# Small tiles move to the constants pool, and the pools behind start at one address offset

## The chip, the cores and the metric

The kernel runs on one core of a Trainium2 chip. The metric is device time in microseconds (us) of one execution, from launch to end; lower is better. The profile shows one execution of the same program, instruction by instruction.

## What is computed

One decoder layer on 512 tokens of width 1024, in float32, plus a final norm:

```
h = x + 0.5 * SwiGLU(RMSNorm(h))            # d_ff 2816
u = RMSNorm(h);  P = u @ W_in               # short conv, Mamba-2 and gate columns
y_a = W_out_a(b * conv3(c * v))
y_b = W_out_ssm(GroupRMSNorm(SSD(conv4(xBC)) * silu(z)))     # 32 heads, 4 groups, chunks of 128
h = h + W_mix_out(sigmoid(g_a) * y_a + sigmoid(g_b) * y_b)
h = h + CrossAttn(RMSNorm(h), RMSNorm(mem))                  # 4 heads, 256 memory tokens
h = h + 0.5 * SwiGLU(RMSNorm(h))
out = RMSNorm(h)
```

## The kernel before

Everything is held transposed: channels on the 128 partitions, the 512 tokens along the free axis. So a tile of one 128-channel block is 128x512 float32, which is 2048 bytes per partition. The output of every weight product is built in PSUM 128 channels at a time.

**The inner loop.** Nearly all of TensorE's time goes to `job` (lines 99 to 112). It computes one 128-channel block of `x @ W`: for each of the k blocks of input channels, a 128x128 block of the weights is the stationary operand and an activation tile of 128x512 is the moving one. To get float32 precision out of the faster float32r matmuls, both operands are split into a high and a low part, and each k block takes three matmuls: high weights with high activations (line 110), high weights with low activations (line 111) and low weights with high activations (line 112). `load_w` (lines 86 to 97) brings 128x1024 weights by DMA (`wr`), ScalarE rounds them to the high part (`wh`, line 84) and VectorE subtracts for the low part (`wl`, line 85); three buffers of each rotate in the pool `wp`.

**The moving tiles** have names that tell the stage. `uh`/`ul` are the layer input with its gain (pool `up`; both feed-forward gate/up products, the projection `w_in`, and the queries). `sh`/`sl` are the SwiGLU products (pool `fp`; both down projections). `ynh`/`ynl` are the normed SSD outputs (pool `mx`; `w_os`). `yah`/`yal` and `mgh`/`mgl` are the short-conv output and the merged branches (pool `mb`; `w_oa` and `w_mo`). `mnh`/`mnl` are the memory tokens (256 wide; `w_k`). For `w_v` (lines 516 to 518) the roles are turned: 512 columns of weights move and `mnh`/`mnl` are stationary. `kh`/`kl` move and `qh`/`ql` are stationary in the attention scores (lines 559 to 561), `ph`/`pl` move against `vh`/`vl` (lines 598 to 600), and `oh`/`ol` are the attention outputs (pool `xo`; `w_o`). The last block of the second down projection is done in two halves of 256 tokens (`finish`, lines 650 to 652).

**Memory.** Pools are laid out one behind the other in SBUF, in the order in which they are opened: `cst` (constants), `wp` (weights), then `up` (u tiles) and `wk` (work tiles `sq`, `sd`, `rc`, `r`, `sdf`), then the pool of the stage (`fp`, `mo` with `mx` or `mb`, `xa` with `xn` or `xo`). The residual tiles `h` sit at the other end. A tile takes its bytes per partition, rounded up to 32. All large tiles are multiples of 1 KB, so a small tile shifts everything behind it: in `wk`, two `sd` and two `rc` buffers (16 bytes, rounded to 32) stand in front of `r` and `sdf` (64 bytes) behind it; in `xo`, four `mxs` buffers (32 bytes) stand in front of `e`, `ph`, `pl`, `oh` and `ol`.

**The order of work** is that of the program on each engine: no instruction is placed by a planner at run time. TensorE works through jobs, with the small products of the SSD and of the norms between them.

Of the kernel before, what the change touches and what calls it, by code (L numbers as in the profile page):

```python
# [16 lines left out]
F32 = mybir.dt.float32  # L17
# [5 lines left out]
P = 128  # L23
# [24 lines left out]
def layer(ctx: ExitStack, tc: tile.TileContext, a, out):  # L48
# [4 lines left out]
    cst = ctx.enter_context(tc.tile_pool(name="cst", bufs=1))  # L53
# [8 lines left out]
    def nm(s):  # L62
        uid[0] += 1
        return f"{s}_{uid[0]}"

    def ps(tag="pj"):
        return psp.tile([P, T], F32, tag=tag, name=nm(tag), bufs=PJ if tag == "pj" else 8 - PJ)
# [7 lines left out]
    eps = cst.tile([P, 1], F32, tag="eps", name="eps")  # L75
    V.memset(eps, EPS)

    ahead = []

    def pc(name, i):  # L80
# [6 lines left out]
    def load_w(src, n, parts=1):  # L87
        if ahead:
            return ahead.pop(0)
        raw = wp.tile([P, 1024], F32, tag="wr", name=nm("wr"), bufs=3)  # L90
        hi = wp.tile([P, 1024], F32R, tag="wh", name=nm("wh"), bufs=3)
        lo = wp.tile([P, 1024], F32R, tag="wl", name=nm("wl"), bufs=3)
        for i in range(parts):
            c = slice(i * n // parts, (i + 1) * n // parts)
            nc.sync.dma_start(out=raw[:, c], in_=src[:, c])
            split(raw[:, c], hi[:, c], lo[:, c])
        return hi, lo
# [25 lines left out]
    def rms(tiles, n, pool, n_tok=T):  # L123


        nt = n_tok // P
        acc = None
        for k, t in enumerate(tiles):
            sq = pool.tile([P, T], F32, tag="sq", name=nm("sq"), bufs=3)[:, :n_tok]
            S.activation(out=sq, in_=t, func=AF.Square)  # L130
            if acc is None:
                acc = sq
            else:
                V.tensor_tensor(out=sq, in0=acc, in1=sq, op=ALU.add)  # L134
                acc = sq
        p1 = ps("ss")
        for c in range(nt):
            TE.matmul(p1[:, c:c + 1], acc[:, c * P:(c + 1) * P], ones[:, 0:1], start=True, stop=True)
        sd = pool.tile([P, 4], F32, tag="sd", name=nm("sd"), bufs=2)[:, :nt]
        S.activation(out=sd, in_=p1[:, :nt], func=AF.Sqrt, scale=1.0 / n, bias=eps)  # L140
        rc = pool.tile([P, 4], F32, tag="rc", name=nm("rc"), bufs=2)[:, :nt]
        V.reciprocal(out=rc, in_=sd)
        rb = pool.tile([P, T], F32, tag="sq", name=nm("rb"), bufs=3)[:, :n_tok]
        V.tensor_copy(out=rb.rearrange("p (c t) -> p c t", c=nt),
                      in_=rc.unsqueeze(2).to_broadcast([P, nt, P]))
        p2 = ps("ss")
        for c in range(nt):
            TE.transpose(p2[:, c * P:(c + 1) * P], rb[:, c * P:(c + 1) * P], ident)
        r = pool.tile([P, T], F32, tag="r", name=nm("r"), bufs=2)[:, :n_tok]
        S.copy(out=r, in_=p2[:, :n_tok])  # L150
        return r
# [12 lines left out]
    wk = ctx.enter_context(tc.tile_pool(name="wk", bufs=1, reuse_waits="tile"))  # L164
# [325 lines left out]
    with tc.tile_pool(name="xa", bufs=1, reuse_waits="tile") as xa:  # L490
# [36 lines left out]
        with tc.tile_pool(name="xo", bufs=1, reuse_waits="tile") as xo:  # L527
            def xt(tag, bufs, shape=(P, T), dt=F32):
                return xo.tile(list(shape), dt, tag=tag, name=nm(tag), bufs=bufs)
# [19 lines left out]
            def scores(hd, qs):  # L549
                pp = [ps("ss") for _ in range(2)]  # L550
                probs = []
                for c2 in range(2):
                    sc = pp[c2]
                    for cc in range(2):
                        cs = slice((2 * c2 + cc) * P, (2 * c2 + cc + 1) * P)
                        o_ = sc[:, cc * M:(cc + 1) * M]
                        for j in range(2):
                            (qh, ql), (kh, kl) = qs[j], kT[2 * hd + j]
                            TE.matmul(o_, qh[:, cs], kh, start=(j == 0), stop=False)  # L559
                            TE.matmul(o_, qh[:, cs], kl, start=False, stop=False)  # L560
                            TE.matmul(o_, ql[:, cs], kh, start=False, stop=(j == 1))  # L561
                    mx_ = xt("mxs", 4, (P, 8))
                    V.tensor_reduce(out=mx_[:, 0:2], in_=sc.rearrange("p (c m) -> p c m", c=2),
                                    op=ALU.max, axis=AX.X)
                    V.tensor_scalar(out=mx_[:, 2:4], in0=mx_[:, 0:2], scalar1=-1.0 / 16, scalar2=None,
                                    op0=ALU.mult)
                    e = xt("e", 2)
                    for cc in range(2):
                        es = slice(cc * M, (cc + 1) * M)
                        S.activation(out=e[:, es], in_=sc[:, es], func=AF.Exp, scale=1.0 / 16,  # L570
                                     bias=mx_[:, 2 + cc:3 + cc], accum_out=mx_[:, 4 + cc:5 + cc])
                    V.reciprocal(out=mx_[:, 6:8], in_=mx_[:, 4:6])
                    for cc in range(2):
                        es = slice(cc * M, (cc + 1) * M)
                        V.tensor_scalar(out=e[:, es], in0=e[:, es], scalar1=mx_[:, 6 + cc:7 + cc],
                                        scalar2=None, op0=ALU.mult)
                    probs.append(e)
                return probs
# [58 lines left out]
    def finish(pool, w, s, r):  # L637
        k7 = KD - 1
        per = 8
        ws = [load_w(w[:, k0 * P:min(KF, k0 + per) * P], (min(KF, k0 + per) - k0) * P)  # L640
              for k0 in range(0, KF, per)]
        ov = out.rearrange("(c p) f -> c p f", p=P)
        sd = wk.tile([P, 16], F32, tag="sdf", name="sdf", bufs=1)
        for half in range(2):
            hs = slice(half * 256, half * 256 + 256)
            pd = ps()
            for k in range(KF):
                hi, lo = ws[k // per]
                c = slice((k % per) * P, (k % per + 1) * P)
                TE.matmul(pd[:, :256], hi[:, c], s[k][0][:, hs], start=(k == 0), stop=False)  # L650
                TE.matmul(pd[:, :256], hi[:, c], s[k][1][:, hs], start=False, stop=False)  # L651
                TE.matmul(pd[:, :256], lo[:, c], s[k][0][:, hs], start=False, stop=(k == KF - 1))  # L652
            if half == 0:
                emit(pool, KD - 2)
            dn = pool.tile([P, T], F32, tag="gt", name=nm("dn"), bufs=2)
            V.scalar_tensor_tensor(out=dn[:, :256], in0=pd[:, :256], scalar=0.5, in1=r[:, hs],
                                   op0=ALU.mult, op1=ALU.mult)
            V.tensor_tensor(out=h[k7][:, hs], in0=dn[:, :256], in1=h[k7][:, hs], op=ALU.add)
            sq = wk.tile([P, T], F32, tag="sq", name=nm("sq"), bufs=3)
            S.activation(out=sq[:, :256], in_=h[k7][:, hs], func=AF.Square)  # L660
            V.tensor_scalar(out=h[k7][:, hs], in0=h[k7][:, hs], scalar1=pc("final_norm", k7),
                            scalar2=None, op0=ALU.mult)
            p1 = ps()
            for j in range(2):
                c = 2 * half + j
                TE.matmul(p1[:, j:j + 1], acc[0][:, c * P:(c + 1) * P], ones[:, 0:1],
                          start=True, stop=False)
                TE.matmul(p1[:, j:j + 1], sq[:, j * P:(j + 1) * P], ones[:, 0:1],
                          start=False, stop=True)
            o2 = slice(2 * half, 2 * half + 2)  # L670
            S.activation(out=sd[:, o2], in_=p1[:, 0:2], func=AF.Sqrt, scale=1.0 / D, bias=eps)
            rc = sd[:, 4 + 2 * half:6 + 2 * half]
            V.reciprocal(out=rc, in_=sd[:, o2])
            pt = ps("ss")
            for j in range(2):
                c = 2 * half + j
                TE.transpose(pt[:, j * P:(j + 1) * P], h[k7][:, c * P:(c + 1) * P], ident)
            for j in range(2):
                c = 2 * half + j
                V.tensor_scalar(out=ot[0][:, c, :k7 * P], in0=ot[0][:, c, :k7 * P],  # L680
                                scalar1=rc[:, j:j + 1], scalar2=None, op0=ALU.mult)
                S.activation(out=ot[0][:, c, k7 * P:], in_=pt[:, j * P:(j + 1) * P], func=AF.Copy,
                             scale=rc[:, j:j + 1])
                (nc.sync if j == 0 else S).dma_start(out=ov[c], in_=ot[0][:, c, :])

    ffn("ffn2_norm", a["w_gu2"], a["w_d2"], finish)


# [59 lines left out]
```

## Time and profile before

| | |
|---|---|
| median of 3 runs | 1626.18 us (1625.16 to 1627.94) |
| profiled execution, its own time | 1626.07 us |
| its span (first to last instruction) | 1624.3 us |
| TensorE busy | 1593.0 us, 98% of the span |
| VectorE, ScalarE, GpSimd busy | 53%, 41%, 3% |
| DMA queues | 168.58 MB, mean 104 GB/s |
| mean granted TensorE clock | 0.995 |

The profiled execution's own time is 1.8 us over its span, and 0.1 us under the median. A matmul's record lasts some 390 ns for 512 columns, but the next one starts after some 230 ns: records overlap, since matmuls are pipelined. So the length of a record does not tell the pace; the distance from start to start does, and it is read from a count of instructions in a stretch or from two start times with the number between them.

### The profile page before, as it was taken

How to read it: one execution, taken by the hardware profiler on the slowest of the kernel's cores; microseconds unless marked ns; L12 is line 12 of the kernel's file. 1: busy time of each engine (PE TensorE's matmuls, PEld its weight loads, DVE VectorE, ACT ScalarE, POOL GpSimd, SP SyncE). 2: the span in 40 equal slices, each digit the busy share in tenths (PEclk: the TensorE clock that was granted, in tenths of full speed). 3: DMA queues.
4: the chain of work that ended last, by engine and by line, in shares of the span. 5: the costliest groups of instructions: out<-in, count | busy, mean ns of one | idle time of the engine just before them, and what ended most of it. 6: DMA issues, size and time to landing. Idle time of an engine off the chain costs nothing.

```text
span 1624.3 us, 18647 instructions
## 1 busy us (share of the span) xinstructions
PE 1593.0 (98%) x7437; PEld 1301.0 (80%) x7437; DVE 856.4 (53%) x1134; ACT 660.7 (41%) x888; POOL 52.0 (3%) x54
## 2 busy tenths in 40 slices
PE   8999999999999999999999999999999999999997
PEld 6888888887878777787888888888878888888887
DVE  5434443346695876958565554565555434343333
ACT  6232222224768583775332222344443323232222
POOL 0000000000120100201010000000000000000000
PEclk9999999999999999999999999999999999999999
DMA  5333323333442423423253323235213232333331
GB/s 192 95 100 93 102 89 103 114 107 101 128 123 76 133 85 104 130 91 104 78 194 94 101 91 104 91 103 183 78 30 114 91 102 92 98 97 86 93 97 62
DMA packets 53911, 168.58 MB, mean 104 GB/s; under 512 B 6320, under 2 KB 6832, under 8 KB 53824
## 3 DMA queue, kind: packets, MB, share of 16 engines
q1 hardware_dynamic: 51952, 161.03, 31.9%
q0 software_dynamic: 1584, 5.31, 0.9%
q8 instruction: 58, 0.95, 0.2%
q10 hardware_dynamic: 288, 1.05, 0.2%
q14 instruction: 29, 0.24, 0.0%
HBM read 163.10 MB, written 4.26 MB: 103 GB/s over the span
## 4 chain that ended last, share of the span: by engine, by line
PE 56%; DVE 1%; issue 1%; DMA 1%; ACT 0%; DVEq 0%; ACTq 0%
PE pj L110 17%; PE pj L112 17%; PE pj L111 17%; DMA ea<-acd 1%; PE pj L518 0%; PE pj L517 0%; PE pj L516 0%; PE pj L650 0%; PE pj L652 0%; PE pj L651 0%; PE ss L598 0%; PE ss L379 0%; PE ss L561 0%; PE ss L560 0%; PE ss L559 0%
## 5 line engine op out<-in xcount | busy, mean ns | idle before, releaser
L84 ACT CAST wh<-wr 128x1024 fp32r<-128x1024 f32 (+2 forms) x298 | 294.1, 988 | 801.9 <-PE pj L111 670.1
L110 PE MATMUL pj<-uh,wh 128*128 128x512 f32 x1416 | 557.3, 394 | 6.9 <-ACT wh L84 6.8
L112 PE MATMUL pj<-uh,wl 128*128 128x512 f32 x1416 | 554.9, 392 | 0.0
L111 PE MATMUL pj<-ul,wh 128*128 128x512 f32 x1416 | 554.8, 392 | 0.0
L85 DVE TENSOR_TENSOR wl<-wr,wh 128x1024 fp32r<-128x1024 f32 (+2 forms) x298 | 341.2, 1145 | 199.3 <-ACT wh L84 193.9
L110 PEld LDWEIGHTS pj<-uh,wh 128*128 128x128 f32 x1416 | 266.6, 188 | 63.9 <-ACT wh L84 6.8
L112 PEld LDWEIGHTS pj<-uh,wl 128*128 128x128 f32 x1416 | 266.8, 188 | 57.0 <-issue 0.7
L111 PEld LDWEIGHTS pj<-ul,wh 128*128 128x128 f32 x1416 | 266.9, 188 | 55.8 <-DVE ul L120 0.7
L110 PE MATMUL pj<-sh,wh 128*128 128x512 f32 x330 | 130.6, 396 | 0.0
L112 PE MATMUL pj<-sh,wl 128*128 128x512 f32 x330 | 130.2, 394 | 0.0
L111 PE MATMUL pj<-sl,wh 128*128 128x512 f32 x330 | 130.2, 394 | 0.0
L179 DVE TENSOR_TENSOR gt<-pj,gt 128x512 f32<-128x512 f32 x44 | 30.4, 692 | 137.2 <-PE pj L112 136.5
L177 DVE TENSOR_TENSOR gt<-pj,r 128x512 f32<-128x512 f32 x44 | 30.3, 692 | 113.0 <-PE pj L112 109.5
L112 PEld LDWEIGHTS pj<-sh,wl 128*128 128x128 f32 x330 | 61.8, 187 | 15.3
L111 PEld LDWEIGHTS pj<-sl,wh 128*128 128x128 f32 x330 | 61.8, 187 | 14.8
L110 PEld LDWEIGHTS pj<-sh,wh 128*128 128x128 f32 x330 | 61.8, 187 | 14.8
L221 DVE SCALAR_TENSOR_TENSOR cv<-cx,prm,cv 128x511 f32<-128x511 f32 (+2 forms) x72 | 63.6, 888 | 3.3 <-ACT cv L218 3.0
L362 POOL TENSOR_TENSOR m<-m,keep 128x512 f32<-128x512 f32 x32 | 41.6, 1315 | 314.0 <-DMA m<-acd 294.3
L112 PE MATMUL pj<-ynh,wl 128*128 128x512 f32 x128 | 50.4, 394 | 0.0
L110 PE MATMUL pj<-ynh,wh 128*128 128x512 f32 x128 | 50.4, 394 | 0.0
L111 PE MATMUL pj<-ynl,wh 128*128 128x512 f32 x128 | 50.4, 394 | 0.0
L134 DVE TENSOR_TENSOR sq<-sq,sq 128x512 f32<-128x512 f32 (+1 forms) x47 | 32.0, 680 | 3.5 <-ACT sq L130 2.7
(223 smaller groups left out, 1656.9 us busy)
## 6 DMA issues: line engine op xcount, KB each, us to landing
wr<-in_w_gu SPq DMA_DIRECT2D x87, 512.0 KB, 3.5
wr<-in_w_in SPq DMA_DIRECT2D x80, 512.0 KB, 3.6
wr<-in_w_d SPq DMA_DIRECT2D x32, 512.0 KB, 3.5
m<-acd SPq DMA_DIRECT2D x32, 256.0 KB, 3.8
wr<-in_w_os SPq DMA_DIRECT2D x32, 256.0 KB, 3.0
wr<-in_w_d SPq DMA_DIRECT2D x16, 384.0 KB, 3.1
ea<-acd SPq DMA_DIRECT2D x32, 128.0 KB, 4.4
wr<-in_w_oa SPq DMA_DIRECT2D x8, 512.0 KB, 3.5
```

Source lines behind the costliest of these rows:

```text
L84: S.copy(out=hi, in_=src)
L85: V.tensor_tensor(out=lo, in0=src, in1=hi, op=ALU.subtract)
L110: TE.matmul(pt, hi[:, s_], xh, start=(k == 0), stop=False)
L111: TE.matmul(pt, hi[:, s_], xl, start=False, stop=False)
L112: TE.matmul(pt, lo[:, s_], xh, start=False, stop=(k == nk - 1))
L134: V.tensor_tensor(out=sq, in0=acc, in1=sq, op=ALU.add)
L177: V.tensor_tensor(out=gt, in0=pg, in1=r, op=ALU.mult)
L179: V.tensor_tensor(out=gt, in0=pu, in1=gt, op=ALU.mult)
L221: V.scalar_tensor_tensor(out=acc[:, d:], in0=x[:, :T - d], scalar=pc(wname, j0 + j), in1=acc[:, d:], op0=ALU.mult, op1=ALU.add)
L362: G.tensor_tensor(out=m4, in0=m4, in1=acs[:, (h0 + hh) * NC:(h0 + hh + 1) * NC].unsqueeze(2) .to_broadcast([P, NC, P]), op=ALU.subtract)
```

## The change

`sd`, `rc`, `mxs` and `sdf` are taken out of the working pools and allocated in the constants pool, which lies in front of the weights; `sd`, `rc` and `sdf` get 8 columns (32 bytes) each. An unused tile of 32 bytes, `fill`, is added there too. The instructions, their order on each engine and their waits are the same before and after; only addresses differ.

```diff
@@ -75,6 +75,10 @@
     eps = cst.tile([P, 1], F32, tag="eps", name="eps")
     V.memset(eps, EPS)
 
+
+    cst.tile([P, 8], F32, tag="fill", name="fill")
+    small = lambda tag, n, bufs: cst.tile([P, n], F32, tag=tag, name=nm(tag), bufs=bufs)
+
     ahead = []
@@ -136,9 +140,9 @@
-        sd = pool.tile([P, 4], F32, tag="sd", name=nm("sd"), bufs=2)[:, :nt]
+        sd = small("sd", 8, 2)[:, :nt]
         S.activation(out=sd, in_=p1[:, :nt], func=AF.Sqrt, scale=1.0 / n, bias=eps)
-        rc = pool.tile([P, 4], F32, tag="rc", name=nm("rc"), bufs=2)[:, :nt]
+        rc = small("rc", 8, 2)[:, :nt]
         V.reciprocal(out=rc, in_=sd)
@@ -559,7 +563,7 @@
-                    mx_ = xt("mxs", 4, (P, 8))
+                    mx_ = small("mxs", 8, 4)
@@ -640,7 +644,7 @@
-        sd = wk.tile([P, 16], F32, tag="sdf", name="sdf", bufs=1)
+        sd = small("sdf", 8, 1)
```

In front of the weights this adds 32 (`fill`) + 64 (`sd`) + 64 (`rc`) + 128 (`mxs`) + 32 (`sdf`) = 320 bytes. Behind the weights it takes away 128 bytes before `r`, 64 behind it, and 128 in `xo`. The start addresses per partition, modulo 2048:

| tiles | before | after |
|---|---|---|
| `wr`, `wh`, `wl`, `uh`, `ul`, `sq` | 1568 | 1888 |
| `r` | 1696 | 1888 |
| `gt`, `sh`, `sl`, `yb`, all tiles of `mx` and `mb` (`ynh`, `yah`, `mgh`, ...), `vh`, `vl`, `qh`, `ql` | 1760 | 1888 |
| `mnh`, `mnl`, `kh`, `kl` (1 KB each) | 1760 or 736 | 1888 or 864 |
| `e`, `ph`, `pl`, `oh`, `ol` | 1888 | 1888 |
| `h` (other end of SBUF) | 2016 | 2016 |
| `con` (in front of the small tiles) | 1024 | 1024 |

A 128x128 block of weights starts at a multiple of 512 bytes behind its tile's start.

## Rows read from the trace of the kernel before

**Rows 1.** The head of the page: span, then busy time by engine.
```profile
span 1624.3 us, 18647 instructions
PE 1593.0 (98%) x7437; PEld 1301.0 (80%) x7437; DVE 856.4 (53%) x1134; ACT 660.7 (41%) x888; POOL 52.0 (3%) x54
```
**Rows 2.** Waits of PE: for whom, us in total, times, longest.
```profile
PE ss L379 <- DVE m L367: 9.2, 4, 2.7
PE pj L110 <- ACT wh L84: 6.8, 1, 6.8
PE ss L138 <- DVE sq L134: 3.7, 3, 1.8
```
**Rows 3.** Windows, PE: stretch, length, busy (instructions), PEclk, DMA share, GB/s.
```profile
50.00:250.00 200.00, 200.00 (x884) 1.00 0.31 95
270.00:360.00 90.00, 90.00 (x387) 1.00 0.34 109
514.00:535.00 21.00, 21.00 (x92) 1.00 0.46 140
840.00:950.00 110.00, 110.00 (x487) 1.00 0.32 101
1044.00:1060.00 16.00, 16.00 (x70) 1.00 0.30 95
1090.00:1106.00 16.00, 16.00 (x144) 1.00 0.58 174
1108.00:1128.00 20.00, 20.00 (x89) 1.00 0.60 188
1217.00:1245.00 28.00, 28.00 (x124) 1.00 0.39 117
```
**Rows 4.** Timeline of PE, 954 to 966 us: start, length; first matmul of three jobs.
```profile
954.48 0.39 PE L110 MATMUL pj<-yah,wh 128*128 128x512 f32 x1
...
960.08 0.39 PE L110 MATMUL pj<-uh,wh 128*128 128x512 f32 x1
...
965.54 0.39 PE L110 MATMUL pj<-yah,wh 128*128 128x512 f32 x1
```
**Rows 5.** Groups of PE by form: shapes, count, busy us, mean ns, idle before.
```profile
L110 PE MATMUL pj<-uh,wh 128*128 128x512 f32 x1408 | 554.1, 394 | 6.9 <-ACT wh L84 6.8
L110 PE MATMUL pj<-sh,wh 128*128 128x512 f32 x330 | 130.6, 396 | 0.0
...
L110 PE MATMUL pj<-ynh,wh 128*128 128x512 f32 x128 | 50.4, 394 | 0.0
...
L110 PE MATMUL pj<-mgh,wh 128*128 128x512 f32 x64 | 25.4, 397 | 0.0
...
L110 PE MATMUL pj<-oh,wh 128*128 128x512 f32 x64 | 25.3, 397 | 0.0
L110 PE MATMUL pj<-yah,wh 128*128 128x512 f32 x64 | 25.2, 394 | 0.0
...
L110 PE MATMUL pj<-mnh,wh 128*128 128x256 f32 x64 | 17.5, 278 | 1.3 <-ACT mnh L84 1.3
```
**Rows 6.** Timeline of PE, attention scores: the first and last of 17 starts.
```profile
1153.09 0.28 PE L559 MATMUL ss<-kh,qh 128*128 128x256 f32 x1
...
1155.01 0.28 PE L560 MATMUL ss<-kl,qh 128*128 128x256 f32 x1
```
**Rows 7.** Timeline of PE, second half of the last block: first and last of 54 starts.
```profile
1608.28 0.28 PE L650 MATMUL pj<-sh,wh 128*128 128x256 f32 x1
...
1614.52 0.28 PE L652 MATMUL pj<-sh,wl 128*128 128x256 f32 x1
```

## The prediction

> **What bounds the kernel now.** I read the head of the page first: TensorE is busy for 1593.0 of 1624.3 us, while VectorE and ScalarE have about half of their time free [rows 1]. Then the waits of TensorE: the largest sum is 9.2 us, for VectorE's product `m` in the SSD, then 6.8 us once for the first weights, and 3.7 us for the norm's sum of squares [rows 2]. So nearly everywhere the time is the number of matmuls times the distance from one start to the next. Transfers do not bound it: in most of the stretches the DMA engines are busy for about a third of the time, at most 0.60 [rows 3].
>
> The third view is a table of stretches, each filled with one kind of matmul [rows 3]. The count takes in the matmul that lies over the front edge, so the distance from start to start is (stretch + length of one record) / count, with 0.39 us for 512 columns and 0.28 us for 256. All stretches are at a granted clock of 1.00, the 2.4 GHz level, and TensorE is busy through each of them. Yet matmuls of one shape go at different paces:
>
> - u tiles, at 50 and at 840 us: 200.39/884 = 226.7 ns, and 110.39/487 = 226.7 ns.
> - `sh` of the down projection, at 270 us: 90.39/387 = 233.6 ns; `ynh` at 514 us: 21.39/92 = 232.5; `mgh` at 1044 us: 16.39/70 = 234.1.
> - `w_v`, at 1108 us: 20.39/89 = 229.1 ns; `oh`, at 1217 us: 28.39/124 = 229.0.
> - `mnh`, 256 columns, at 1090 us: 16.28/144 = 113.1 ns.
>
> The short counts are good to one instruction, 1%. The difference is sharper where two kinds take turns: around 960 us a job of 24 matmuls on `yah` takes 960.08 - 954.48 = 5.60 us, 233.3 ns each, and the next job of 24 on `uh`, the same code and shapes, 965.54 - 960.08 = 5.46 us, 227.5 ns each [rows 4].
>
> What else differs between these kinds is the address. Take the distance of the moving tile's start from the stationary tile's start, modulo 256 bytes (weight blocks step by 512, so the block does not matter). For the u tiles it is 1568 - 1568 = 0. For `sh`, `ynh`, `yah`, `mgh` it is 1760 - 1568 = 192. For `oh` it is 1888 - 1568 = 320, so 64. For `w_v` it is 1568 - 1760, again 64. So distance 0 goes with 226.7 ns, 64 with 229 ns (in two stages with different tiles in either role), 192 with 233.3 ns. That two different pairs with distance 64 agree is my reason to take the distance, and not an address by itself, as the cause.
>
> **The change part by part.** No instruction is added, removed or moved, and no wait. The new addresses bring every one of these pairs to distance 0: moving tiles and weights both start at 1888 modulo 2048, or 864 for half of the 1 KB tiles. With distance as the cause, each 512-column matmul goes to 226.7 ns. Counts are three times the rows of line 110 [rows 5], or come from the loops:
>
> - `sh`/`sl`: 3 x 330 = 990, at 6.6 ns each: 6.5 us. TensorE does not wait in either down projection, so all of it reaches the end.
> - `mgh`/`mgl` and `yah`/`yal`: 2 x 3 x 64 = 384, at 6.6 ns: 2.5 us, equally on the path.
> - `ynh`/`ynl`: 3 x 128 = 384, at 6.6 ns: 2.5 us, between the SSD groups. There VectorE prepares the next group meanwhile, and TensorE waits 9.2 us in all for its `m` [rows 2]. Where it arrives earlier it may only wait longer. Bounds 0 and 2.5; I take half, 1.3 us.
> - `oh`/`ol`: 3 x 64 = 192 at 2.3 ns, 0.4 us. `w_v`: 2 x 8 x 2 x 3 = 96 at 2.4 ns, 0.2 us. `ph`/`pl` against `vh`/`vl` are 48 matmuls at distance 128, between 0 and 6.6 ns each: 0 to 0.3 us, I take 0.2.
> - The 4224 u matmuls (3 x 1408) keep distance 0, but both addresses move from 1568 to 1888. If only the distance counts this costs nothing. They are the large lever: 4.2 us for each nanosecond. No row shows 512 float32r columns below 226.7, so I see no gain; the upper bound is the slowest pace of the table, 6.6 ns or 28 us. I take nothing, by the nearest rows, since u matmuls at 50 and 840 us agree to 0.1 ns.
> - 256 columns: the only such pairs at distance 0 are the scores, (1155.01 - 1153.09)/16 = 120.0 ns [rows 6]. `mnh` at distance 192 goes at 113.1 and will come to distance 0: 3 x 64 = 192 matmuls at 6.9 ns, 1.3 us lost. The last block's second half goes at (1614.52 - 1608.28)/53 = 117.7 ns [rows 7]; if its first half goes like `mnh`, at 113, the mean is 115.4, and 2 x 22 x 3 = 132 matmuls at 4.6 ns lose 0.6 us. Scores alternate products more often than jobs do, so the loss may be none: bounds 0 and 1.9 us, I take 1.9.
> - The small tiles themselves are read and written by the same instructions at another place; their work is a few operations per norm and per head, and I cost it at nothing. The cover is that TensorE has other matmuls during most norms; without it, their price could at most lengthen waits like the 3.7 us of [rows 2].
>
> Sum: 6.5 + 2.5 + 1.3 + 0.4 + 0.2 + 0.2 = 11.1 us gained, 1.9 us lost, net 9.2 us. The profiled execution's own time was 1626.07 us, which makes 1616.9; the median of the runs lies 0.1 us above it. I predict 1617 us.
>
> Against this stands a rule of the Trainium skill, TensorE: Matmul & The Clock Gate, section "Step-by-step: what each phase is for": the moving operand and the weight load have two independent read ports, and loading the next weights takes no read bandwidth from the running matmul. By that rule no pair of addresses could cost more than another and the sum would be 0. The trace does not agree with its plain reading: 233.3 beside 227.5 ns in neighbouring jobs [rows 4]. It would hold if something other than the address sets the pace.
>
> **The rivals.**
>
> *The pace does not belong to addresses.* Then it belongs to the stage (what the other engines do meanwhile, the order of the jobs), and nothing changes: 1626 us. For it: the second half of the last block goes at 117.7 ns and `mnh` at 113.1 with the same distance modulo 256, so the distance is not the whole story. Against it: `yah` and `uh` jobs take turns in one stage. Chance 0.12.
>
> *The moving tile's own address counts.* The only moving tiles now at 1888 against weights are `oh`, and they go at 229.0 ns. If 1888 by itself gives that pace, the u matmuls lose 4224 x 2.3 = 9.7 us, the 990 + 384 + 384 at distance 192 gain 1758 x 4.3 = 7.6 us, and the 256-column ones lose up to 1.9: 4 us slower, 1630 us. Its place is the gate/up products and `w_in`; it decides as soon as their spacing rises over 226.7 + 9.2/4.2 = 228.9 ns, where the gain of the rest is eaten. Against it: `w_v` has its moving tile at 1568, like the u matmuls, and goes at 229.1. Chance 0.14. In its worst form, 233.3 ns for all u matmuls, it costs 28 us less the 1.6 us or so left elsewhere: about 1652 us, chance 0.04.
>
> *The matmuls get faster, the end does not.* TensorE is then held by something that was hidden: the splits of weights or the SSD's chain. If only the down projections gain, 6.5 us, and the 1.9 us are lost, it is 4.6 us: about 1621.5 us. Against it: no waits in the other stages, and `wh`, `wl` and transfers have room [rows 1, 3]. Chance 0.08.
>
> **How the numbers follow.** The forecast has 0.62, with its own range 1613 (all gains, no loss at 256 columns, nothing lost in the SSD) to 1620 us. What can be told from no change is 0.2%, 3.3 us, so faster means under 1622.9 us and slower over 1629.4. Faster: the forecast and nearly all of the last rival, 0.70. Same: the first rival and the lower edge of the second, 0.14. Slower: the second in its two forms, 0.16. The range 1612 to 1630.5 us holds the forecast, the case of no change, and about half of the second rival; it leaves out the worst form and the ends.
>
> **What would show it right or wrong.** Right: in windows of the profile after, `sh`, `ynh`, `mgh`, `yah`, `oh` and `w_v` all go at 226.7 ns, u matmuls stay there, and `mnh` rises to 120. The second rival shows as u matmuls at 229 ns or more. The first shows as `yah` jobs still at 5.60 us beside `uh` jobs at 5.46. If `ynh` goes at 226.7 but TensorE's wait for `m` rises over 9.2 us, the half that I dropped is lost. A change of the times without a change of these distances from start to start would mean that my whole account is wrong.

## The result, and the profile after

The changed kernel takes 1614.27 us (median of 4 runs, 1613.39 to 1614.92) against 1625.67 us for the kernel before, run beside it (4 runs, 1622.51 to 1627.94). The ratio is 0.9931, with a 95% interval of 0.9913 to 0.9949: about 11 us faster, where 9.2 were forecast. The profiled execution after took 1613.93 us by its own time, and its span is 12.1 us shorter than before.

The head of the page after, span and busy time by engine, answers to [rows 1]:

```profile
span 1612.2 us, 18647 instructions
PE 1583.2 (98%) x7437; PEld 1305.2 (81%) x7437; DVE 853.6 (53%) x1134; ACT 660.3 (41%) x888; POOL 50.8 (3%) x54
```

Every count is the same as before, and no engine but TensorE is anywhere near full. The busy time of TensorE fell by 9.8 us (1593.0 - 1583.2). Work that is neither added nor taken away, on the same engine, has become shorter.

The waits of TensorE after (for whom, us in total, times, longest) answer to [rows 2]:

```profile
PE ss L383 <- DVE m L371: 9.0, 4, 2.6
PE pj L114 <- ACT wh L88: 7.0, 1, 7.0
PE ss L142 <- DVE sq L138: 2.1, 3, 1.1
```

The three sums are 9.0 + 7.0 + 2.1 = 18.1 us, against 9.2 + 6.8 + 3.7 = 19.7. So most of the 12 us is not waiting, and no wait has grown into their place. But TensorE's idle time as a whole did fall, from 1624.3 - 1593.0 = 31.3 us to 1612.2 - 1583.2 = 29.0, and 1.6 us of that is the wait for the norms' sum of squares `sq`; these waits all lie in the SSD stage.

The windows of TensorE after (stretch, length, busy and count, granted clock, DMA share, GB/s) answer to [rows 3]. In order they hold u, `sh`, `ynh`, u, `mgh`, `mnh`, `w_v`, `oh`:

```profile
50.00:250.00 200.00, 200.00 (x884) 1.00 0.31 96
270.00:360.00 90.00, 90.00 (x399) 1.00 0.36 111
509.00:529.00 20.00, 20.00 (x90) 1.00 0.45 138
840.00:944.00 104.00, 104.00 (x461) 1.00 0.31 97
1040.00:1055.00 15.00, 15.00 (x68) 1.00 0.35 107
1079.00:1095.00 16.00, 16.00 (x136) 1.00 0.52 164
1100.00:1118.00 18.00, 18.00 (x81) 1.00 0.59 188
1206.00:1234.00 28.00, 28.00 (x125) 1.00 0.36 113
```

With the formula of the prediction, (stretch + one record) / count, the 512-column kinds are now alike:

| kind | distance before | ns before | distance after | ns after |
|---|---|---|---|---|
| u, 50 us | 0 | 226.7 | 0 | 226.7 |
| `sh` | 192 | 233.6 | 0 | 226.5 |
| `ynh` | 192 | 232.5 | 0 | 226.6 |
| u, 840 us | 0 | 226.7 | 0 | 226.4 |
| `mgh` | 192 | 234.1 | 0 | 226.3 |
| `w_v` | 64 | 229.1 | 0 | 227.0 |
| `oh` | 64 | 229.0 | 0 | 227.1 |
| `mnh`, 256 columns | 192 | 113.1 | 0 | 119.7 |

The clearest row of all is the pair of job kinds that take turns. The timeline of TensorE after, first matmul of three successive jobs of 24, answers to [rows 4]:

```profile
945.32 0.39 PE L114 MATMUL pj<-yah,wh 128*128 128x512 f32 x1
...
950.76 0.39 PE L114 MATMUL pj<-uh,wh 128*128 128x512 f32 x1
...
956.20 0.39 PE L114 MATMUL pj<-yah,wh 128*128 128x512 f32 x1
```

Both jobs now take 5.44 us; before, `yah` took 5.60 beside 5.46 for `uh`.

The last block's second half after (start, length; first and last of 54 starts) answers to [rows 7]:

```profile
1596.05 0.28 PE L654 MATMUL pj<-sh,wh 128*128 128x256 f32 x1
...
1602.40 0.28 PE L656 MATMUL pj<-sh,wl 128*128 128x256 f32 x1
```

(1602.40 - 1596.05)/53 = 119.8 ns, against 117.7. So 256 columns became slower, as the windows show for `mnh`.

To see where the span went I paired every matmul of one trace with its twin in the other and summed the differences from start to start. By kind: `sh` -6.4 us, `ynh` -2.6, `yah` -1.3, `mgh` -1.2, `oh` -0.3, `ph` -0.2, `w_v` -0.2, u 0.0 in both gate/up products (in the first from 50 us on); `mnh` +2.7 and the last block +0.5. That is -9.0. The remaining 3 us lie between the other instructions of the SSD stage (395 to 830 us in the trace before); the section on the prediction says what they are.

### The profile page after: what moved, and what is told of

It is laid out like the page before. It is cut to its first block, busy times and chain, and to the rows that moved or that the text cites. A ratio compares the mean times of both kernels' runs of the same rounds, so it can differ in the third digit from the quotient of the medians.

```text
span 1612.2 us, 18647 instructions
## 1 busy us (share of the span) xinstructions
PE 1583.2 (98%) x7437; PEld 1305.2 (81%) x7437; DVE 853.6 (53%) x1134; ACT 660.3 (41%) x888; POOL 50.8 (3%) x54
## 4 chain that ended last, share of the span: by engine, by line
PE 57%; issue 1%; DVE 1%; ACT 0%; DMA 0%; DVEq 0%; ACTq 0%
PE pj L114 17%; PE pj L116 17%; PE pj L115 17%; PE pj L520 0%; PE pj L521 0%; PE pj L522 0%; PE ss L383 0%; PE pj L654 0%; PE pj L656 0%; PE pj L655 0%; PE ss L388 0%; DMA m<-acd 0%; PE ss L602 0%; PE ss L565 0%; PE ss L564 0%
```

## The experiments

All start from the changed kernel and only move addresses; the work stays the same. "Distance" is the moving tile's start minus the stationary tile's start, modulo 256 bytes unless a larger number is given; D is the theory that this distance sets the spacing. Unused tiles (`pad`) move what lies behind them.

**1. All starts back at 1568: not the place, the distance.** The small tiles go to a pool at the other end of SBUF, so that weights and moving tiles meet at 1568 rather than 1888.

```diff
+    smp = ctx.enter_context(tc.tile_pool(name="smp", bufs=1, side="right"))
-    cst.tile([P, 8], F32, tag="fill", name="fill")
-    small = lambda tag, n, bufs: cst.tile([P, n], F32, tag=tag, name=nm(tag), bufs=bufs)
+    small = lambda tag, n, bufs: smp.tile([P, n], F32, tag=tag, name=nm(tag), bufs=bufs)
```

> The small tiles lie at the far end of SBUF beside h, so that the weights stay at 1568 modulo 2048 as in the kernel before, and all moving tiles lie at 1568 too (h shifts from 2016 to 1728). Theory D (the distance between moving and stationary start sets the spacing): every distance is 0, so 226.7 ns for all 512-column jobs, 120 ns for 256 columns, and the same time as the changed kernel, 1614 us within 2. Theory A (the address itself counts; 1888 is a good place, or 1760 and 1888 bad ones): sh, ynh, yah and mgh need not come to 226.7; if the place is what counts, some of the 11 us are missing, 1618 to 1626 us. Theory S (the moved small tiles themselves give the gain): 1614 us too, but sh would then not depend on the pads of the other kernels of this call.

Measured: 1613.86 us (4 runs, 1612.26 to 1616.36) against 1624.94, ratio 0.9935, interval 0.9919 to 0.9952. The windows of TensorE in this run, u, `sh`, `ynh`, `oh`:

```profile
50.00:250.00 200.00, 200.00 (x884) 1.00 0.31 95
270.00:360.00 90.00, 90.00 (x399) 1.00 0.37 111
512.00:532.00 20.00, 20.00 (x90) 1.00 0.46 134
1208.00:1234.00 26.00, 26.00 (x117) 1.00 0.40 122
```

The counts for `sh` and `ynh` repeat those of the changed kernel, and `oh` goes at 26.39/117 = 225.6 ns (good to one instruction, 2 ns). `oh`, which did not move in the change, got faster there because its weights moved; here its own tile moved back with them, and it is as fast. So neither 1568 nor 1888 is good or bad by itself, and the place of the small tiles does nothing either.

**2 to 4. Other distances, one run each.** A pad at the front of each working pool puts each kind at its own distance. These are the tiles added in run 2 (the lines between them and the condition that limits the first to one down projection are left out); runs 3 and 4 have other sizes (in bytes: 128 in the first `fp`, 160, 192, 128, 96; and 224, 256, 320, 192, 160).

```diff
+    fp.tile([P, 8], F32, tag="pad", name=nm("pad"))    # first down projection only
+    mx.tile([P, 16], F32, tag="pad", name=nm("pad"))
+    mb.tile([P, 24], F32, tag="pad", name=nm("pad"))
+    xm.tile([P, 16], F32, tag="pad", name=nm("pad"))
+    xo.tile([P, 8], F32, tag="pad", name=nm("pad"))
```

> The changed kernel with an unused tile in front of a stage's pool, so that the distance to the weights, modulo 512, is 32 for sh of the first down projection (528 matmuls), 64 for ynh (384), 96 for yah and mgh (384), 64 for mnh (192, 256 columns), and 32 for oh and for the pairs of the scores. Theory D, from the three values of the kernel before (0: 226.7, 64: 229, 192: 233.3 ns): about 228 ns at 32, 229 at 64, 230.5 at 96; together 528 x 1.3 + 384 x 2.3 + 384 x 3.8 ns, some 3 us over the changed kernel, 1617 us. The second down projection stays at distance 0 and at 226.7. Theory A: no relation to the distance is expected, and ynh at 1952 may be anything. Theory S: 226.7 everywhere, 1614 us.

> As the kernel before it in this call, with distances 128 for sh of the first down projection, 160 for ynh, 192 for yah and mgh, 128 for mnh, 96 for oh. Theory D: 231.5 ns at 128, 232.5 at 160 and the 233.3 of the kernel before at 192 although the addresses are others (yah at 32 instead of 1760); together 528 x 4.8 + 384 x 5.8 + 384 x 6.6 ns less what the SSD hides, 6 to 7 us over the changed kernel, 1620.5 us. Theory A: yah at 32 modulo 2048 has no reason to repeat 233.3. Theory S: 226.7 everywhere, 1614 us.

> As the kernel before it in this call, with distances 224 for sh of the first down projection, 256 for ynh, 320 for yah and mgh, 192 for mnh, 160 for oh. Theory D with a period of 256 bytes: ynh back at 226.7 ns, yah and mgh at the 229 of distance 64, sh at 224 at 233 or more, mnh back at 113 as in the kernel before; together about 528 x 6.6 + 384 x 2.3 ns less 1.3 us for mnh, 3 us over the changed kernel, 1617 us. Theory D with a period of 512: ynh at 256 need not be 226.7, and 320 stays at 229 (w_v and oh lay there). Theory A: no relation. Theory S: 226.7 everywhere, 1614 us.

Measured: 1624.95, 1627.58 and 1621.43 us. Windows of the first (`sh` at 32, `ynh` at 64, `mgh` at 96, `oh` at 32):

```profile
270.00:360.00 90.00, 90.00 (x387) 1.00 0.34 107
514.00:534.00 20.00, 20.00 (x89) 1.00 0.44 137
1052.00:1067.00 15.00, 15.00 (x66) 1.00 0.34 107
1216.00:1244.00 28.00, 28.00 (x121) 1.00 0.37 113
```

Windows of the second (`sh` at 128, `ynh` at 160, `mgh` at 192):

```profile
270.00:360.00 90.00, 90.00 (x387) 1.00 0.35 107
517.00:537.00 20.00, 20.00 (x87) 1.00 0.43 138
1053.00:1068.00 15.00, 15.00 (x66) 1.00 0.32 107
```

Windows of the third (`sh` at 224, `ynh` at 256, `mgh` at 320, `mnh` at 192, `w_v` at 64):

```profile
270.00:360.00 90.00, 90.00 (x388) 1.00 0.34 106
515.00:535.00 20.00, 20.00 (x90) 1.00 0.47 141
1048.00:1063.00 15.00, 15.00 (x67) 1.00 0.31 101
1085.00:1101.00 16.00, 16.00 (x138) 1.00 0.53 165
1106.00:1124.00 18.00, 18.00 (x79) 1.00 0.58 181
```

Worked out as before, the spacing of 512 columns is 233.6 ns at 32, 229.1 at 64, 233.2 at 96, 233.6 at 128, 234.4 at 160, 233.2 at 192, 233.0 at 224, 226.6 at 256 and 229.7 at 320. So the period of 256 that the prediction assumed holds, and 192 repeats the pace of before at other addresses. My times for the runs, 1617, 1620.5 and 1617, were 4 to 8 us too low. In runs 2 and 3 this was in part because I had taken the distances between the known ones from a straight line: 528 x 5.6 + 384 x 2.7 ns = 4 us of the 8 in run 2, but 528 x 2.1 + 384 x 1.9 ns = 1.8 of the 7 in run 3. There is no line: 0 is a narrow dip, and 32 bytes beside it cost as much as 128. My sums had also left out `oh`, which goes at 28.39/121 = 234.6 ns at 32 bytes (run 2), 1.4 us more than in the changed kernel. What else went into these misses, with one run each, is open. In run 4 the line had no part. Two rows there do not fit the distance alone: `w_v` at 64 goes at 18.39/79 = 232.8 ns, not 229, and `mnh` at 192 at 16.28/138 = 118.0, not 113.1. Run 8 follows these up, and run 7 the width of the dip.

**5. All moving tiles 128 bytes off the weights.** A pad in front of the u tiles moves them and all pools behind by 128 bytes, so those pools still share one offset; only the weights lie at another. That separates the words of the change (one offset for all pools behind) from the distance.

```diff
+    up.tile([P, 32], F32, tag="pad", name="pad")
```

> The changed kernel with 128 unused bytes in front of the u tiles, so that u tiles and everything behind lie at 2016 and the weights stay at 1888: distance 128 for every job, the 4224 u matmuls too, with all pools behind the weights still at one offset. Theory D (distance to the weights): 233.3 ns, as sh had at distance 128, for all 4224 + 990 + 384 + 384 + 192 + 96 = 6270 matmuls against weights, 6.6 ns each, 41 us over the changed kernel: 1655 us, perhaps some us less where the SSD hides it. The scores and the probabilities times v, whose two operands move together, stay at 120 and 226.7 ns. Theory O (it is enough that the pools behind the weights share one offset among themselves, or that small tiles no longer break them up): 1614 us. Theory A (the moving tile's own address): 2016 has not been tried, between 1614 and 1655 us.

Measured: 1648.37 us (4 runs, 1647.72 to 1649.74) against 1625.96, ratio 1.0145, interval 1.0128 to 1.0162. The windows of this run, u in all three:

```profile
50.00:250.00 200.00, 200.00 (x859) 1.00 0.30 92
860.00:960.00 100.00, 100.00 (x432) 1.00 0.30 94
1300.00:1490.00 190.00, 190.00 (x819) 1.00 0.30 95
```

One unused tile of 128 bytes costs 34 us against the changed kernel, 34.7 us by the spans (1646.9 - 1612.2). That a common offset of the working pools would be enough is refuted. By itself this run can't tell the distance from the new place, 2016. For the distance speaks that 192 gave the same pace with other addresses (233.3 before, 233.2 in run 3), and that `oh`, whose own tile is at 1888 before and after, went from 229.0 to 227.1 ns when only its weights moved. The u matmuls go at 233.3 ns at 50 us and 232.4 and 232.5 in the later stretches (100.39/432 and 190.39/819), so the size stayed below the 41 us that I gave (6.6 ns for all); why the later ones are a nanosecond better I can't say.

**6. Without `fill`.** The weights and all behind lie 32 bytes lower, at 1856.

```diff
-    cst.tile([P, 8], F32, tag="fill", name="fill")
```

> The changed kernel without the unused 32-byte tile in front: weights and all moving tiles at 1856 instead of 1888, every distance 0. Theory D: the same spacings, 226.7 ns, and 1614 us within 2: that tile does nothing. Theory A: 1856 is a multiple of 64, which no offset tried so far was; if that counts, u matmuls leave 226.7 ns and the time moves by 4.2 us for each ns.

Measured: 1615.46 us (4 runs, 1613.55 to 1616.68) against 1625.96, ratio 0.9939, interval 0.9918 to 0.9960. Its windows, u and `sh`, have the counts of the changed kernel:

```profile
50.00:250.00 200.00, 200.00 (x884) 1.00 0.31 96
270.00:360.00 90.00, 90.00 (x399) 1.00 0.36 111
```

`fill` does nothing that can be measured. 1856 is a third place at which distance 0 gives 226.5 ns for `sh`.

**7. How narrow the dip is (one run).** Wider tiles are read from a column further in: `sh` at 16 bytes, `yah` at 8, `ynh` at 4.

```diff
-                hi = fp.tile([P, T], F32R, tag=f"sh{ct}", name=nm("sh"))
-                lo = fp.tile([P, T], F32R, tag=f"sl{ct}", name=nm("sl"))
+                w_, o_ = (T + 64, 4) if fin is None else (T, 0)
+                hi = fp.tile([P, w_], F32R, tag=f"sh{ct}", name=nm("sh"))[:, o_:o_ + T]
+                lo = fp.tile([P, w_], F32R, tag=f"sl{ct}", name=nm("sl"))[:, o_:o_ + T]
...
-                hi, lo = mt("ynh", 4, dt=F32R), mt("ynl", 4, dt=F32R)
+                hi, lo = (mt(n_, 4, (P, T + 64), F32R)[:, 1:1 + T] for n_ in ("ynh", "ynl"))
...
-            hi, lo = wt("yah", 8, F32R), wt("yal", 8, F32R)
+            hi, lo = (mb.tile([P, T + 64], F32R, tag=n_, name=nm(n_), bufs=8)[:, 2:2 + T] for n_ in ("yah", "yal"))
```

> The changed kernel with tiles 256 bytes longer, of which the matmuls use a part that starts behind the tile's start: distance 16 bytes for sh of the first down projection (528 matmuls), 4 for ynh (384), 8 for yah (192); all others at 0. Theory D with a smooth dip: spacings between 226.7 and the 233 of distance 32, about 230 at 16, 227.5 at 4, 228.3 at 8. Theory D with a sharp dip (0 or a multiple of 256 and nothing else): 233 ns for all three, 528 + 384 + 192 matmuls at 6.6 ns, 7 us: 1621 us. If 226.7 is not the lowest spacing there is, one of the three lies below it. That distance 0 is not special at all, only multiples of 16 bytes: 226.7 at 16 and another value at 4 and 8.

Measured: 1623.89 us, where I had 1621 for a sharp dip. Windows of `sh` and `ynh`:

```profile
270.00:360.00 90.00, 90.00 (x390) 1.00 0.34 107
512.00:532.00 20.00, 20.00 (x86) 1.00 0.44 132
```

And the timeline of its alternating jobs, as above:

```profile
953.82 0.40 PE L114 MATMUL pj<-yah,wh 128*128 128x512 f32 x1
...
959.42 0.39 PE L114 MATMUL pj<-uh,wh 128*128 128x512 f32 x1
...
964.89 0.40 PE L114 MATMUL pj<-yah,wh 128*128 128x512 f32 x1
```

At 16 bytes the spacing is 231.8 ns, at 8 bytes (959.42 - 953.82)/24 = 233.3 beside 227.9 for `uh`, at 4 bytes 20.39/86 = 237.1, the slowest 512-column pace of any run. So already the smallest step off zero loses the gain. What 237.1 and 233.3 owe to the distance alone stays open for 4 and 8 bytes: their tiles do not start at a multiple of 16 bytes, and this run can't tell that from the distance.

**8. The 256-column loss taken back.** Run 1 with a pad of 192 bytes that puts `mnh`, and the weights that meet it in `w_v`, at the addresses that they had before.

```diff
+            xm.tile([P, 48], F32, tag="pad", name=nm("pad"))
```

> The kernel with everything at 1568 (small tiles at the far end), with 192 unused bytes in front of the memory tokens only: mnh and mnl at 1760 and 736, as in the kernel before, where 256 columns went at 113.1 ns, against 117.7 at distance 192 with other addresses (mnh at 32, weights at 1888). Theory D for 256 columns (the distance alone): as the second finding had the same distance, 113 or 117.7, it can't say which. Theory P (at 256 columns the place itself counts beside the distance): 113.1 ns again since both addresses are those of the kernel before, and w_v, which reads mnh as its stationary operand, at 229 again. Then 192 x 6.8 ns = 1.3 us are won and 96 x 2.4 ns = 0.2 us lost against the kernel with everything at 1568: 1613 us, the fastest so far, by less than one comparison can tell. If neither returns (117.7 and 233), what decides at distances other than 0 is not the two start addresses modulo 2048.

Measured: 1613.5 us (6 runs, 1609.83 to 1615.08) against 1624.6, ratio 0.9926, interval 0.9911 to 0.9942. The window of `mnh`, and the first and last of 43 starts in `w_v` on the timeline:

```profile
1078.00:1094.00 16.00, 16.00 (x144) 1.00 0.52 160
```

```profile
1099.99 0.39 PE L521 MATMUL pj<-wh,mnh 128*128 128x512 f32 x1
...
1109.60 0.39 PE L521 MATMUL pj<-wh,mnh 128*128 128x512 f32 x1
```

`mnh` is back at 113.1 ns and `w_v` at 9.61/42 = 228.8. In run 4 the same distances stood at other places (`mnh` at 32 and not 224 modulo 512, the weights at 352 and not 32) and gave 118.0 and 232.8. So away from zero something of the addresses besides this distance decides too, which the prediction's two numbers for distance 64 could not show. It is not the two starts modulo 512 either: `oh` before had its moving tile at 352 and its stationary one at 32, like `w_v` in run 4, and went at 229.0. The stretch of `mnh` is within 0.02 us of before, but the sum gains nothing that can be measured.

**9. The changed kernel once more, beside run 8**, with no edit.

> The changed kernel once more, on the same chip as the run beside it, for a second measure of the ratio to the kernel before and of how much its SSD stage (395 to 830 us) varies between executions: in the profiles so far it took 5.5 us less than before in the one and 4.0 us less in the other kernel with all distances 0, of which 2.6 us are the ynh matmuls. Theory D: 226.7 ns in all stages outside, a median of 1614 us, and a gain there of 2.6 us plus a rest that may have either sign. If the rest is again -1.4 us or more, the SSD gains something that my sum did not have.

Measured: 1613.02 us (5 runs, 1611.84 to 1613.34), ratio 0.9928, interval 0.9916 to 0.9940. Runs 8 and 9 can't be told apart, so no version here is shown to beat the changed kernel. The SSD stage was 5.4 us shorter than before, 2.9 us beyond `ynh`. That passes the mark of 1.4 us which I had set for a gain that my sum did not have; what the 2.9 us consist of stands in the next section.

## Why the prediction was right, step by step

**The mechanism** held. Distance 0 gives 226.7 ns at 1568, 1856 and 1888 (runs 1, 6 and the change) and at 256 (run 4); other distances give 229 to 237; and run 5 puts the same tiles 128 bytes off and loses 34 us with no other edit.

**The terms at 6.6 and 2.3 ns.** `sh` 6.5 forecast, 6.4 measured. `yah` and `mgh` 2.5, measured 1.3 + 1.2. `oh` 0.4, measured 0.3. `w_v` and `ph` 0.2 each, and so measured. The u matmuls moved from 1568 to 1888 at no cost, as forecast from the nearest rows.

**`ynh`, the half that I dropped.** This was mis-sized: 1.3 us forecast, 2.6 measured. I had expected TensorE to arrive earlier at `m` and to wait longer for it. That wait is 9.0 us after and 9.2 before (9.1, 9.5, 9.2 and 9.0 in runs 1, 6, 8 and 9), so these matmuls reach the end in full. The sign I had named for this (the wait rises) did not come.

**The rest of the SSD stage.** It gave 3 us more that were in no term. In four further profiles with all distances of this stage at 0 (runs 1, 6, 8 and 9), the whole stage is 4.0, 3.0, 3.2 and 5.4 us shorter than in the one profile of before; `ynh` is 2.56 us of this each time. So the rest is 0.4 to 3.0 us for equal paces. The stage before, after and in run 9:

```profile
395.12:830.03 434.91, 420.99 (x2066) 0.99 0.36 112
```

```profile
391.49:820.88 429.39, 417.92 (x2066) 0.99 0.36 114
```

```profile
390.45:819.92 429.47, 416.32 (x2067) 0.99 0.36 114
```

TensorE idles 434.91 - 420.99 = 13.9 us of it before and 11.5 after: 2.5 of the 3.0 us are waits. In run 9, the same kernel, it idles 13.2 us, but the clock falls to half for 3.4 us only twice in the stage (at 458 and 574 us), while it does so three times both before (464, 580 and 679 us) and after (556, 651 and 672 us). One such piece costs about 1.4 us where `mnh` met it (below), so 0.8 + 1.4 = 2.2 of run 9's 2.9 us are accounted for, by this estimate. In runs 1, 6 and 8 idle time and half-clock pieces leave at most 0.7 us in the same way. The u matmuls inside the jobs of this stage stay 227.7 and 227.8 ns apart before and after, with stretches at half clock and distances over 300 ns left out. So the rest is no faster pace but mostly waiting and time at half clock, and these differ between two profiles of one kernel too (after and run 9). The wait for `sq` alone is 3.7 us before, 2.1 after, and 5.0, 3.3, 2.8 and 3.4 in runs 1, 6, 8 and 9. Whether the new addresses have any share in it, one profile of before can't tell. Whole executions scatter with the clock too: of the 25 runs of the kernel before that were made beside the experiments, those with a mean clock of 0.994 have a median of 1625.8 us (6 runs), those with 0.995 1624.8 (12) and those with 0.996 1623.3 (4).

**256 columns.** `mnh` lost 2.7 us where I had 1.3. The spacing came as forecast, 119.7 ns for 120.0, and explains 1.3. The other 1.4 us are a piece of 3.4 us of this stretch at half clock. TensorE after, that piece, and then all 192 matmuls of `mnh`:

```profile
1074.50:1077.90 3.40, 3.40 (x19) 0.52 0.51 154
1072.65:1098.18 25.53, 24.86 (x192) 0.93 0.46 145
```

The same 192 before, and in run 1:

```profile
1084.38:1107.19 22.81, 22.14 (x192) 1.00 0.52 161
```

```profile
1074.71:1098.77 24.06, 23.39 (x192) 1.00 0.49 154
```

A granted clock of 0.52 is nearly the 1.2 GHz level of the two (1.00 is 2.4 GHz). Ahead of it TensorE waited 1.3 us for `mnh` and, some matmuls later, 0.7 us for `mnl`. It did so before and in run 1 too, and there the clock stayed at 1.00, and run 1 lost 24.06 - 22.81 = 1.25 us. Such a fall just behind these two waits stands in 7 of the 11 profiles (after and runs 3, 4, 5, 6, 7 and 9) and not in the other four (before and runs 1, 2 and 8). `mnh` at distance 0 has it in run 6 and not in run 1, at distance 192 in run 4 and not before. So the distance alone doesn't decide it; whether the addresses change how often it comes, eleven profiles don't tell. The last block lost 0.5 us, forecast 0.6.

**The sum.** The terms came to 9.0 us against 9.2 forecast, but not because each was right: `ynh` gave 1.3 us more and `mnh` lost 1.4 us more than I had, and that these two cancel is luck. The median moved by 11.4 us; the 2.4 beyond the terms are of the size of the rest of the SSD stage.

**The rivals.** That the pace belongs to the stage fell with the alternating jobs: 5.44 us for both kinds. That the moving tile's own address counts fell with u at 1888 (226.7 ns), and with `oh` at 1568 in run 1. That the end would not follow fell with the waits, which did not grow. The rule of the Trainium skill (TensorE: Matmul & The Clock Gate, section "Step-by-step: what each phase is for"), that loading the next weights takes no read bandwidth from the running matmul, would have made the sum 0 if it covered where the two tiles start. Here it does not: between run 5 and the change only such addresses differ, and 512 columns go at 233.3 and 226.7 ns at 50 us. Whether the loss is in a read port or somewhere else no run shows.

**What the range rested on.** The argument assumed a mechanism from three distances (0, 64 and 192), and for runs 2 to 4 I guessed that the values between them lie on a line. For the forecast it was enough that all pairs go to a distance already seen, 0. The forecasts for other distances, in runs 2 to 4, were off by 4 to 8 us, at most about half of it by that line.

## What to carry to other kernels

Where TensorE is nearly always busy and one shape goes at several paces, compare the start addresses of the moving and the stationary tiles: here, for 512 float32r columns, starts that agree modulo 256 bytes gave 226.7 ns and all others that were tried 229 to 237; run 5, where the 6270 matmuls against weights lost that agreement, took 34 us more than 1614. A small tile at the front of a pool shifts everything behind it, so an edit that adds or drops one can move the time of matmuls that it never touches; small tiles in front of the weights did no harm here, nor did they at the other end. A pace read at a few distances should not be drawn as a line to the next.

## What was unexpected of the hardware

- The dip is narrow: 226.7 ns at 0 and 256, 231.8 at 16, 233.6 at 32; 237.1 at 4 and 233.3 at 8, where the start at no multiple of 16 bytes may count too.
- 256 columns go the other way: 119.7 ns at distance 0, 118.0 at 192 at one place and 113.1 at 192 at another (runs 4 and 8). What decides there is open.
- Distance 64 (or 320) gave 229 ns in four pairs and 232.8 in one (`w_v` in run 4).
- An unused pad of 128 bytes, in a kernel that is otherwise the same, made it 2.1% slower (1648.37 against 1614.27 us), at a clock of 1.00 in each stretch shown.
- TensorE fell to half clock for some 3 us behind two short waits (1.3 and 0.7 us) in 7 of 11 profiles of almost the same program, and in the other four the same waits left it at 1.00.
